# Queries and keys loaded apart, FFN units woven in halves, and TensorE in the program's order

## The chip, the cores and the metric

The kernel runs on one core of a Trainium2 chip. A core has five engines that work side by side and meet at semaphores: TensorE (PE, matmuls; PEld is its loading of weights), VectorE (DVE), ScalarE (ACT), GpSimd (POOL) and SyncE (SP), which here only issues DMAs. Each engine takes its own instructions strictly in the order in which they were put into its queue: a waiting instruction holds up all that stand behind it. Matmul results land in PSUM, of which the program uses eight banks of 128 x 512 float32; everything else is in SBUF or, beyond the core, in HBM. The metric is the device time of one execution in microseconds (us).

## The reference

One layer over 2048 time steps of 1024 channels, all in float32:

```python
h = _rmsnorm(x, g_attn)
p = h @ w_in                      # parts a_b, a_c, a_h, b_glu, q, k, v
y_a = a_b * _causal_dwconv(a_c * a_h, w_conv_a)
g = b_glu[..., :256] * jax.nn.sigmoid(b_glu[..., 256:])
y_b = jax.nn.silu(_layernorm(_causal_dwconv(g, w_conv_b) + b_conv_b, ...))
y_c = _stick_breaking(q, k, v)    # 8 heads of 64
x = x + jnp.concatenate([y_a, y_b, y_c], axis=-1) @ w_out
h2 = _rmsnorm(x, g_ffn)
x = x + jnp.square(jax.nn.relu(h2 @ w_ff1)) @ w_ff2
return _rmsnorm(x, g_final)
```

Stick-breaking attention has no softmax. With the scores z = q k / 8, a key s < t gets the weight sigmoid(z[t, s]) times the product of sigmoid(-z[t, r]) over the keys r between s and t. The kernel needs running products over keys, from the latest backwards.

## The kernel before, in words

Every float32 product is made of three faster ones: a factor is split into a rounded high part and the rest (lo), and TensorE adds high x high, lo x high and high x lo. `mm3` (lines 99 to 107) emits these, so lines 103, 105 and 107 stand for all large products; PSUM tiles tell them apart (ps_p input projection, ps_x output projection, ps_u first FFN product, ps_y second, ps_z scores, ps_o attention's output).

Time runs along the free axis in four blocks of 512 steps (TB). The first part, up to about 600 us, makes the input projection, the two convolution mixers and the attention of block 0, and writes keys and queries to HBM (KQ) and values (VS). The second part is four calls of `block(tb, ...)`: output projection (eight tiles ps_x, 24 matmuls each), the norm, then 32 units `ffn1` (24 matmuls each) and, after every four of them, `ffn2` (eight tiles ps_y of 12 matmuls). Weights come in pieces through buffers w1 (four pieces, two units) and w2 (three); block 0 splits w1 and stores the parts, block 1 does so for w2, and later blocks load them.

Attention for block i + 1 runs beside block i. `attention` (line 702) is a generator over groups (head h, block i). It mixes two passes, one step at a time: `a_pass1` of a group and `a_pass2` of the group before. A step of pass 1 makes one PSUM tile of scores (ps_z), two sigmoids on ACT, and products on POOL and DVE. The first three steps are the diagonal block, made from `Kd`, the block's own keys, with masks on POOL (`a_diag`); then come 4 i steps with the earlier keys `Kl`, which have one buffer and whose load is issued at the head's first step. `a_cross_a` (line 603) then makes the running products across partitions: a transposition of 32 x 32 squares into T, a scan into O, small products C, and a product back into T. A step of pass 2 multiplies a tile A0 with transposed products (ps_q), splits it into Ahi (ACT) and Alo (POOL), and two steps later issues the matmuls with values into ps_o (`a_av`, lines 691 to 700).

`weave` (line 57) sets how the two mix. Main generators yield their cost (5.2 per unit of 24 matmuls, 2.6 per ps_y tile), and after each yield the side generator is driven on to a share of its own cost (0.5 per step) that grows from 0 at `t0` = 45 to its whole at `t1` = 365 or 320. So in the program's text attention's instructions stand in clumps between units. That text is only a priority: a scheduler, which runs a model of the timeline, then fixes each engine's queue, taking ready instructions first by priority (`high_priority` moves some forward). The order on the chip is fixed before it runs.

`a_load` (line 489) brings KQd: a tile of three parts (keys, high queries, low queries), issued on POOL's queue, with one buffer (`KQd=1`); in `attention` it is called after a group's loop has ended. In `block`, lines 955 to 966 take the column sum of squares (ps_ss) by TensorE, form mt on DVE, spread it by TensorE over partitions (ps_R), copy it to ms, and scale the eight tiles acc by it before the first `ffn2` adds to them.

## Time and profile before

| what | value |
|---|---|
| median of 3 runs | 2451.35 us (2446.44 to 2455.63) |
| the profiled execution | 2458.28 us, its span 2456.6 us |
| mean granted TensorE clock | 0.990 of full speed |
| instructions in the span | 32414 |
| data moved | 549.05 MB, 224 GB/s on the mean |
| HBM read and written | 390.38 MB and 148.11 MB |

A row of a group reads: line, engine, operation, what it writes and reads, shapes and count; then busy time and mean time of one in ns; then the idle time of the engine before it and what ended that. A windows row gives, for a stretch of the span, its length, the busy time of PE, PEld, DVE, ACT and POOL with the number of instructions, the granted TensorE clock (1.00 is full speed), the share of the 16 DMA engines that was busy, and GB/s. A timeline row gives start and duration in us. A busy TensorE need not be at its peak, since matmuls overlap in their records.

### The profile page before, as it was taken

The numbers are of one execution on the slowest core, as the hardware profiler recorded it, in microseconds if no ns is written. First come the engines' busy times: TensorE is split into PE (matmuls) and PEld (weight loads), VectorE is DVE, ScalarE is ACT, GpSimd is POOL, SyncE is SP. The second block draws the span as 40 slices with busy tenths as digits, with TensorE's granted clock in tenths as the row PEclk, the third lists the DMA queues.
The fourth block names the chain that finished last, engine by engine and source line by source line (L and its number), as shares of the span: only waits on it lengthen the run. The fifth ranks groups of instructions, "written<-read, shape, count | busy, mean of one in ns | idle before, by whom it ended". The sixth has DMA issues, their size and how long they took to land.

```text
span 2456.6 us, 32414 instructions
## 1 busy us (share of the span) xinstructions
PE 2395.6 (98%) x11316; PEld 2017.3 (82%) x11316; DVE 1627.6 (66%) x2348; ACT 1033.6 (42%) x1910; POOL 1163.9 (47%) x1221
## 2 busy tenths in 40 slices
PE   8999998999999999999999999999999999999998
PEld 7889876898778878787878888888888888888887
DVE  7957799943988878767977768677666735212114
ACT  5232522333566556534545555345555532121121
POOL 1342576641667666515666677158888830000000
PEclk9999999999999999999999999999999999999999
DMA  7579977888688878687778777776666656655555
GB/s 262 189 257 333 298 247 208 239 280 265 161 244 226 230 196 211 175 287 234 218 211 250 241 231 212 243 240 190 183 204 194 199 178 204 242 195 186 200 187 189
DMA packets 236036, 549.05 MB, mean 224 GB/s; under 512 B 25696, under 2 KB 99424, under 8 KB 217440
## 3 DMA queue, kind: packets, MB, share of 16 engines
q1 hardware_dynamic: 162896, 464.11, 54.8%
q0 software_dynamic: 53888, 73.42, 15.8%
q10 hardware_dynamic: 19088, 9.44, 1.3%
q8 instruction: 90, 1.47, 0.2%
q14 instruction: 74, 0.61, 0.1%
HBM read 390.38 MB, written 148.11 MB: 219 GB/s over the span
## 4 chain that ended last, share of the span: by engine, by line
PE 81%; DVE 9%; DMA 6%; issue 2%; ACT 1%; POOL 1%; POOLq 0%; SPq 0%; DVEq 0%; ACTq 0%
PE ps_y L103 8%; PE ps_y L107 8%; PE ps_y L105 8%; PE ps_u L103 8%; PE ps_u L105 8%; PE ps_u L107 8%; PE ps_p L107 4%; PE ps_p L105 4%; PE ps_p L103 4%; DMA KQd<-KQ 2%; PE ps_z L515 2%; PE ps_x L103 2%; PE ps_x L105 2%; PE ps_x L107 2%; PE ps_z L516 2%; DMA w<-s_w 2%
## 5 line engine op out<-in xcount | busy, mean ns | idle before, releaser
L90 POOL TENSOR_TENSOR Alo<-A,Ahi 128x512 fp32r<-128x512 f32 x288 | 394.3, 1380 | 105.7 <-PE ps_o L700 45.9
L944 DVE TENSOR_TENSOR acc<-acc,ps_y 128x512 f32<-128x512 f32 (+1 forms) x264 | 174.8, 666 | 178.0 <-PE ps_y L107 176.6
L103 PE MATMUL ps_y<-fh,w 128*128 128x512 f32 (+1 forms) x1056 | 282.9, 386 | 6.9 <-DVE acc L944 4.5
L103 PE MATMUL ps_u<-hh,w 128*128 128x512 f32 x1024 | 280.2, 394 | 7.7 <-DMA w<-s_w 4.8
L107 PE MATMUL ps_y<-fl,w 128*128 128x512 f32 (+1 forms) x1056 | 279.6, 385 | 1.0 <-DVE fl L919 1.0
L105 PE MATMUL ps_y<-fh,w 128*128 128x512 f32 (+1 forms) x1056 | 279.6, 385 | 0.0
L105 PE MATMUL ps_u<-hh,w 128*128 128x512 f32 x1024 | 278.0, 393 | 0.0
L595 POOL TENSOR_TENSOR A<-A,R 128x512 f32<-128x512 f32 x168 | 232.5, 1385 | 93.7 <-ACT A L593 69.6
L107 PE MATMUL ps_u<-hl,w 128*128 128x512 f32 x1024 | 276.6, 391 | 0.0
L909 ACT ACTIVATE ps_u<-ps_u 128x512 f32<-128x512 f32 x128 | 74.7, 584 | 460.0 <-PE ps_u L107 460.0
L118 POOL TENSOR_TENSOR rs_y<-rs_v,mhalf 128x4 f32<-128x4 f32 (+1 forms) x13 | 14.9, 1149 | 522.0 <-DVE rs_v L117 485.1
L103 PEld LDWEIGHTS ps_y<-fh,w 128*128 128x128 f32 x1056 | 193.2, 188 | 46.7 <-DVE acc L944 4.9
L103 PEld LDWEIGHTS ps_u<-hh,w 128*128 128x128 f32 x1024 | 191.5, 190 | 47.2 <-DMA w<-s_w 6.1
L107 PEld LDWEIGHTS ps_y<-fl,w 128*128 128x128 f32 x1056 | 195.6, 189 | 40.6 <-DVE fl L919 1.6
L105 PEld LDWEIGHTS ps_u<-hh,w 128*128 128x128 f32 x1024 | 194.3, 190 | 41.4 <-DVE w L90 0.2
L105 PEld LDWEIGHTS ps_y<-fh,w 128*128 128x128 f32 x1056 | 195.4, 188 | 39.7
L107 PEld LDWEIGHTS ps_u<-hl,w 128*128 128x128 f32 x1024 | 193.1, 189 | 40.2
L88 ACT ACTIVATE Ahi<-A 128x512 fp32r<-128x512 f32 x288 | 177.5, 628 | 92.9 <-PE ps_o L699 37.0
L919 DVE TENSOR_TENSOR fl<-ps_u,fh 128x512 fp32r<-128x512 f32 x128 | 87.5, 685 | 194.6 <-ACT fh L918 194.2
L597 DVE TENSOR_TENSOR R<-ps_z,R 128x512 f32<-128x512 f32 x168 | 115.4, 687 | 147.8 <-ACT ps_z L594 108.9
L452 DVE SCALAR_TENSOR_TENSOR ps_c<-g,wb,ps_c 128x512 f32<-128x512 f32 x240 | 179.8, 749 | 4.8
L88 ACT ACTIVATE w<-wraw 128x512 fp32r<-128x512 f32 x152 | 92.1, 628 | 182.4 <-PE ps_y L107 115.8
(173 smaller groups left out, 4952.2 us busy)
## 6 DMA issues: line engine op xcount, KB each, us to landing
w<-s_w SPq DMA_DIRECT2D x200, 512.0 KB, 3.5
w<-s_w SPq DMA_DIRECT2D x68, 1024.0 KB, 4.8
wraw<-in_w SPq DMA_DIRECT2D x192, 256.0 KB, 4.9
w<-s_w_out SPq DMA_DIRECT2D x64, 512.0 KB, 4.8
s_w<-w SPq DMA_DIRECT2D x32, 1024.0 KB, 5.5
s_w<-w SPq DMA_DIRECT2D x56, 512.0 KB, 5.2
KQd<-KQ POOLq DMA_DIRECT2D x64, 384.0 KB, 7.1
xraw<-in_xT SPq DMA_DIRECT2D x48, 256.0 KB, 4.8
```

Source lines behind the costliest of these rows:

```text
L88: nc.scalar.activation(hi, x, AF.Copy)
L90: e.tensor_tensor(lo, x, f(hi), op=ALU.subtract)
L103: self.nc.tensor.matmul(ps, wh, xh, start=start and k == 0, stop=False)
L105: self.nc.tensor.matmul(ps, wl, xh, start=False, stop=False)
L107: self.nc.tensor.matmul(ps, wh, xl, start=False, stop=stop and k == n - 1)
L452: nc.vector.scalar_tensor_tensor(t, g[:, k : k + TB], self.wb[:, c, k : k + 1], t, op0=ALU.mult, op1=ALU.add)
L515: nc.tensor.matmul(z[:, oc], keys, g["qh"][:, qc], start=k == 0, stop=False)
L595: nc.gpsimd.tensor_tensor(t, t, R, op=ALU.mult)
L597: nc.vector.tensor_tensor(Rn, z, R, op=ALU.mult)
L909: nc.scalar.activation(ps, ps, AF.Relu)
L919: nc.vector.tensor_tensor(lo, ps, f(hi), op=ALU.subtract)
L944: nc.vector.tensor_tensor(acc[d][:, cols], acc[d][:, cols], ps, op=ALU.add)
```

## The change

It has five edits.

1. `a_load` becomes `a_queries` (tile Qd, two buffers, loads issued on SP's queue) and `a_keys` (tile Kd, one buffer, still on POOL's queue). In `attention` the next group's queries are loaded once the present group has made one step of pass 1, its keys once it has made three.
2. The diagonal products of keys stay in the tile om instead of going to a tile Rd, and are transposed in two halves of 256 columns into T, as soon as each exists. The scan runs in place in T, and the tile O is gone. T1, the diagonal's T, has two buffers in the first part and one in the blocks.
3. `ffn1` yields after each half of a unit (12 matmuls, cost 2.6).
4. In `block` the third unit, `ffn1(2)`, is emitted between the column sum and the spread.
5. The four blocks are built in a region in which TensorE issues its instructions in the order in which the program emits them. The other engines' order, and TensorE's order outside the region, stay the scheduler's.

```diff
-    def a_load(self, h, i):
-        q0 = TB * i
-        pool = self.at
-        g = {"h": h, "i": i}
-        t = pool.tile([P, 3, TB], F32R, name="KQd", tag="KQd", bufs=self.ab["KQd"])
+    def a_queries(self, h, i):
+        q0 = slice(TB * i // 2, TB * i // 2 + TB // 2)
+        q = self.at.tile([P, 2, TB], F32R, name="Qd", tag="Qd", bufs=2)
         for rows, kq in self.kq_halves(h):
-            to = t[rows].rearrange("c a (j q) -> c (a j) q", j=2)
-            self.load_r(to, kq.rearrange("c a j q -> c (a j) q")[:, :, q0 // 2 : (q0 + TB) // 2])
-        g["Kd"], g["qh"], g["ql"] = t[:, 0], t[:, 1], t[:, 2]
-        return g
+            self.dma(q[rows].rearrange("c a (j q) -> c (a j) q", j=2), kq[:, 1:3].rearrange("c a j q -> c (a j) q")[:, :, q0])
+        return {"h": h, "i": i, "qh": q[:, 0], "ql": q[:, 1]}
+
+    def a_keys(self, g):
+        q0 = slice(TB * g["i"] // 2, TB * g["i"] // 2 + TB // 2)
+        g["Kd"] = self.at.tile([P, TB], F32R, name="Kd", tag="Kd", bufs=1)
+        for rows, kq in self.kq_halves(g["h"]):
+            self.load_r(g["Kd"][rows].rearrange("c (j q) -> c j q", j=2), kq[:, 0, :, q0])
...
-        nc.vector.tensor_tensor(Rd[:, lo], om[:, lo], om[:, hi2], op=ALU.mult)
+        nc.vector.tensor_tensor(om[:, hi2], om[:, lo], om[:, hi2], op=ALU.mult)
+        T = pool.tile([P, 16, 33], F32, name="T", tag="T1", bufs=ab["T1"])
+        nc.gpsimd.memset(T[:, :, 32:33], 0.0)
+        nc.vector.transpose(T[:, 0:8, 0:32], om[:, hi2])
...
-        nc.vector.tensor_tensor(Rd[:, hi2], om[:, hi2], R[:, hi2], op=ALU.mult)
+        nc.vector.tensor_tensor(om[:, hi2], om[:, hi2], R[:, hi2], op=ALU.mult)
+        nc.vector.transpose(T[:, 8:16, 0:32], om[:, hi2])
...
-        O = pool.tile([P, 16, 33], F32, name="O", tag="O", bufs=1)
-        nc.vector.tensor_tensor_scan(fl(O), fl(T), fl(self.d1), 1.0, op0=ALU.mult, op1=ALU.add)
+        nc.vector.tensor_tensor_scan(fl(T), fl(T), fl(self.d1), 1.0, op0=ALU.mult, op1=ALU.add)
...
-                if not loaded and self.ab["KQd"] > 1 and d1 >= n1 / 2 and n + 1 < len(groups):
-                    nxt = self.a_load(*groups[n + 1])
-                    loaded = True
-            if not loaded and n + 1 < len(groups):
-                nxt = self.a_load(*groups[n + 1])
+                if nxt is None and d1 >= 1 and n + 1 < len(groups):
+                    nxt = self.a_queries(*groups[n + 1])
+                if nxt and "Kd" not in nxt and d1 >= 3:
+                    self.a_keys(nxt)
...
                     self.mm3(ps, [(*w(d), hh[d], hl[d]) for d in range(4 * q, 4 * q + 4)], start=q == 0, stop=q == 1)
+                    if q == 0:
+                        yield 2.6
...
-            yield 5.2 * len(cs)
+            yield 2.6 * len(cs)
...
+        yield from ffn1(2)
+        need2(2)
         ms = hp.tile([P, TB], F32, name="ms", tag="ss", bufs=2)
...
-        for c in range(2, FC):
+        for c in range(3, FC):
             yield from ffn1(c)
...
-                self.ab = dict(KQd=1, Kl=1, A0=6, om=2, R=1, Alo=2, Ahi=2, Vl=1, late=1, yc=2)
+                self.ab = dict(Kl=1, A0=6, om=2, R=1, T1=2, Alo=2, Ahi=2, Vl=1, late=1, yc=2)
...
-                self.ab = dict(KQd=1, Kl=1, A0=15, om=2, R=2, Alo=3, Ahi=3, Vl=2, late=2, yc=1)
+                self.ab = dict(Kl=1, A0=15, om=2, R=2, T1=1, Alo=3, Ahi=3, Vl=2, late=2, yc=1)
...
-                for tb in range(4):
-                    weave(self.block(tb, self.end), [(at, (74, 95, 107)[tb], 45, 365 if tb < 2 else 320, False)] if tb < 3 else [])
+                with tc.manual_schedule(engines={mybir.EngineType.PE}):
+                    for tb in range(4):
+                        weave(self.block(tb, self.end), [(at, (74, 95, 107)[tb], 45, 365 if tb < 2 else 320, False)] if tb < 3 else [])
```

More of the change, by code (lines that the diff above doesn't have):

```diff
@@ L552, in a_pass1 @@
         A0 = g["A0"] = []
-        Rd = new("Rd", 1)
         k2 = [g["Kd"][:, 0:P], g["Kd"][:, 256 : 256 + P]]
@@ L574, in a_pass1 @@
         nc.gpsimd.tensor_tensor(t, t, R, op=ALU.mult)
-        nc.vector.tensor_tensor(Rd[:, hi2], om[:, hi2], R[:, hi2], op=ALU.mult)
+        nc.vector.tensor_tensor(om[:, hi2], om[:, hi2], R[:, hi2], op=ALU.mult)
+        nc.vector.transpose(T[:, 8:16, 0:32], om[:, hi2])
         A0.append(t)
         yield 1
-        tot = self.a_cross_a(g, Rd, None)
+        tot = self.a_cross_a(g, T, None)
         if not i:
@@ L600, in a_pass1, with a_cross_a @@
             yield 1
-        self.a_cross_a(g, R, tot)
-    def a_cross_a(self, g, R, seed):
-        nc, pool = self.nc, self.at
-        T = pool.tile([P, 16, 33], F32, name="T", tag="T1" if seed is None else "T2", bufs=1)
+        T = pool.tile([P, 16, 33], F32, name="T", tag="T2", bufs=1)
         nc.gpsimd.memset(T[:, :, 32:33], 0.0)
         nc.vector.transpose(T[:, :, 0:32], R)
-        O = pool.tile([P, 16, 33], F32, name="O", tag="O", bufs=1)
+        self.a_cross_a(g, T, tot)
+    def a_cross_a(self, g, T, seed):
+        nc = self.nc
         fl = lambda x: x.rearrange("p a b -> p (a b)")[:, ::-1]
-        nc.vector.tensor_tensor_scan(fl(O), fl(T), fl(self.d1), 1.0, op0=ALU.mult, op1=ALU.add)
+        nc.vector.tensor_tensor_scan(fl(T), fl(T), fl(self.d1), 1.0, op0=ALU.mult, op1=ALU.add)
         C = self.tiny.tile([P, 16], F32, name="C", tag="C", bufs=3)
@@ L618, in a_cross_a @@
             s, d = slice(32 * a + 32, 32 * a + 64), slice(32 * a, 32 * a + 32)
-            nc.vector.tensor_tensor(C[d], C[s], O[s, :, 0], op=ALU.mult)
+            nc.vector.tensor_tensor(C[d], C[s], T[s, :, 0], op=ALU.mult)
         tot = None
@@ L622, in a_cross_a @@
             tot = self.tiny.tile([32, 16], F32, name="tot", tag="tot", bufs=2)
-            nc.vector.tensor_tensor(tot, C[0:32], O[0:32, :, 0], op=ALU.mult)
-        qt = T[:, :, 0:32]
-        nc.vector.tensor_tensor(qt, O[:, :, 1:33], C.unsqueeze(2).to_broadcast([P, 16, 32]), op=ALU.mult)
+            nc.vector.tensor_tensor(tot, C[0:32], T[0:32, :, 0], op=ALU.mult)
+        qt = T[:, :, 1:33]
+        nc.vector.tensor_tensor(qt, qt, C.unsqueeze(2).to_broadcast([P, 16, 32]), op=ALU.mult)
         g["qd" if seed is None else "ql"] = qt
@@ L703, in attention @@
         prev = None
-        nxt = self.a_load(*groups[0])
+        nxt = self.a_queries(*groups[0])
+        self.a_keys(nxt)
         for n in range(len(groups) + 1):
@@ L714, in attention @@
             lag = 0 if prev and prev["i"] else 2
-            loaded = False
             while live1 or live2:
@@ L730, in attention @@
                         live1 = False
-                if not loaded and self.ab["KQd"] > 1 and d1 >= n1 / 2 and n + 1 < len(groups):
-                    nxt = self.a_load(*groups[n + 1])
-                    loaded = True
-            if not loaded and n + 1 < len(groups):
-                nxt = self.a_load(*groups[n + 1])
+                if nxt is None and d1 >= 1 and n + 1 < len(groups):
+                    nxt = self.a_queries(*groups[n + 1])
+                if nxt and "Kd" not in nxt and d1 >= 3:
+                    self.a_keys(nxt)
             prev = g
```

## The prediction

> **What bounds the kernel now.** I read the page first: busy shares, then the chain that ended last.
>
> ```profile
> PE 2395.6 (98%) x11316; PEld 2017.3 (82%) x11316; DVE 1627.6 (66%) x2348; ACT 1033.6 (42%) x1910; POOL 1163.9 (47%) x1221
> PE 81%; DVE 9%; DMA 6%; issue 2%; ACT 1%; POOL 1%; POOLq 0%; SPq 0%; DVEq 0%; ACTq 0%
> PE ps_y L103 8%; PE ps_y L107 8%; PE ps_y L105 8%; PE ps_u L103 8%; PE ps_u L105 8%; PE ps_u L107 8%; PE ps_p L107 4%; PE ps_p L105 4%; PE ps_p L103 4%; DMA KQd<-KQ 2%; PE ps_z L515 2%; PE ps_x L103 2%; PE ps_x L105 2%; PE ps_x L107 2%; PE ps_z L516 2%; DMA w<-s_w 2%
> ```
>
> TensorE (PE) carries 81% of the chain. The number of its matmuls does not change, so the change can win only what TensorE loses: it stands idle for 2456.6 - 2395.6 = 61 us of the span, and it runs some stretches at a lower clock. One transfer has a place of its own in the chain: KQd, a head's block of queries and keys.
>
> Next I read the stages. The edits act mostly in the blocks, from 600 us on; attention ends near 2020. The first row is the windows view of that stage (length, then busy time per engine, granted clock, DMA share, GB/s), the others the waits of TensorE in it (total, times, longest).
>
> ```profile
> 600.00:2020.00 1420.00, 1389.70 (x6311) 1164.90 (x6310) 1056.31 (x1493) 742.71 (x1384) 893.91 (x936) 0.99 0.74 217
> PE ps_z L515 <- DMA KQd<-KQ: 15.2, 6, 5.5
> PE ps_y L103 <- DVE acc L944: 4.5, 4, 2.6
> PE ps_u L103 <- DMA w<-s_w: 3.6, 3, 2.1
> PE ps_u L103 <- DVE acc L944: 2.3, 1, 2.3
> PE ps_y L103 <- DVE fl L919: 2.2, 2, 1.6
> PE ps_y L107 <- DVE fl L919: 1.0, 2, 0.7
> ```
>
> So TensorE is idle for 30.3 us there, and half of it, 15.2 us, is one wait: the first scores of a head (ps_z) for KQd. Then the five windows around the longest of these waits:
>
> ```profile
> 710.00:730.00 20.00, 18.91 (x90) 15.56 (x89) 18.17 (x24) 9.32 (x17) 12.52 (x17) 1.00 1.00 229
> 800.00:820.00 20.00, 18.13 (x84) 15.31 (x83) 16.14 (x20) 10.68 (x20) 12.98 (x17) 0.91 0.68 187
> 880.00:900.00 20.00, 15.73 (x65) 12.72 (x64) 15.10 (x22) 10.65 (x21) 10.38 (x13) 0.91 1.18 252
> 1170.00:1190.00 20.00, 18.05 (x84) 15.37 (x83) 16.93 (x22) 7.96 (x16) 11.58 (x15) 0.91 1.03 238
> 1220.00:1240.00 20.00, 14.48 (x63) 12.07 (x62) 15.21 (x20) 7.09 (x14) 9.35 (x13) 0.88 1.04 296
> ```
>
> The idle times, 1.09 + 1.87 + 4.27 + 1.95 + 5.52 = 14.7 us, are nearly the whole wait. After four of the five the granted clock (0.91, 0.91, 0.91, 0.88) shows a second loss: (0.09 + 0.09 + 0.09 + 0.12) x 20 = 7.8 us of full-speed time, part of it while TensorE stood still anyway.
>
> **The change part by part.** *The loads.* Before, one buffer holds a head's keys and queries, so its load can be issued only when the previous head's last scores are done. The tile view of KQd (issue time, issue to landing) and one piece of the chain:
>
> ```profile
> L83 POOL DMA_DIRECT2D KQd<-KQ x64: 651/688/951, 188.9 to 1905.8; - x64
> DMA to landing us min/median/max: 4.4/7.1/16.8
> 1219.64 16.23 DMA KQd<-KQ
> ```
>
> After, the queries (two buffers) are asked for after the first step of the head before, and the diagonal keys (one buffer) after its third, when their last reader has been issued. A head with i = 1 has 7 first-pass steps, so at least four of them, over half a head, lie between the keys' load and their use, against a median landing of 7.1 us and a worst of 16.8. The waits in the windows at 800 and 880 belong to heads two apart, so a head spans some 40 us there, and half of one is 20. I therefore remove the wait whole: **15.2 us**, and **6 us** of the 7.8 of clock (bounds 0 and 7.8; nearer the upper, since the lowered clock follows the wait). The 64 query loads now go past SP's queue, among weight loads that wait for buffers; SP's own issue has 0% of the chain, and the queries have a whole head of lead. The 64 loads that stay on POOL's queue carry a third of the bytes; POOL's time for one is 0.69 us at most, as now.
>
> [...]
>
> *The tiles T, Rd and O.* The scan runs in place and the products stay in om. The count of DVE operations grows by one per head, since one transposition of 512 columns becomes two of 256:
>
> ```profile
> L608 DVE STREAM_TRANSPOSE T<-Rd 128x512 f32<-128x512 f32 x32 | 22.7, 708 | 0.8
> L944 DVE TENSOR_TENSOR acc<-acc,ps_y 128x512 f32<-128x512 f32 x248 | 168.2, 682 | 173.8 <-PE ps_y L107 172.9
> L944 DVE TENSOR_TENSOR acc<-acc,ps_y 128x256 f32<-128x256 f32 x16 | 6.7, 421 | 4.3 <-PE ps_y L107 3.7
> ```
>
> A half transposition is not in the trace. Bounds: nothing extra, or 0.71 us, a whole transposition. The nearest pair of sizes gives 2 x 421 - 682 = 160 ns, which I take. For the 24 heads of the blocks it lies beside a DVE that is idle for 26% of the stage (1056.31 of 1420). For the 8 heads of the first stage I let it count: 8 x 0.16 = **1.3 us**; at 0.71 it would be 5.7. If the cover in the blocks is gone, 24 x 0.16 = 3.8 more. The memset of T1's last column moves ahead of the head's second diagonal step. It and the keys' load can hold POOL:
>
> ```profile
> POOL T L607 <- DVE ps_q L643: 103.1, 45, 6.7
> POOL KQd L83 <- PE ps_z L516: 33.4, 6, 24.0
> ```
>
> Both waits exist already. Behind them on POOL stand the masks and the low halves (Alo), which the second matmul of attention (ps_o) needs two steps later. POOL is busy 893.91 of 1420 us, and no wait of TensorE for POOL is among the six largest, of which the smallest is 1.0 us, so I cost the move at nothing.
>
> *The third FFN unit before the spread.* In the program's order the spread of the norm would stand right behind the column sum that it needs; now 24 matmuls lie between. The scaling of acc then comes earlier than in the old trace, where fl came late behind it: of 2.2 + 1.0 us I take **2 us** (bounds 0 and 3.2).
>
> *TensorE in the program's order, and units in halves.* Inside a block the weave already hands out attention between units. Halves hand it out after 12 matmuls instead of 24, which evens the pieces; I give that nothing (bounds 0 and the 4.5 us that ps_y waits for acc). At the start of a block it matters: the weave gives no attention before 45 units of work, and the output projection is 8 x 5.2 = 41.6, yet the trace shows attention there, put by the scheduler. The full windows at the start of the FFN of blocks 1 and 3, then ps_o's and ps_z's share at blocks 1 and 2:
>
> ```profile
> 1091.00:1124.00 33.00, 28.75 (x129) 23.48 (x128) 29.01 (x38) 14.81 (x27) 19.91 (x22) 0.90 1.00 325
> 2092.00:2112.00 20.00, 18.55 (x89) 15.45 (x88) 8.66 (x15) 5.37 (x9) 0.00 (x0) 1.00 0.82 318
> 1091.00:1124.00 33.00, 4.71 (x20) 3.13 (x20) 0.00 (x0) 0.00 (x0) 0.90 1.00 325
> 1597.00:1619.00 22.00, 2.01 (x7) 1.32 (x7) 0.68 (x1) 0.59 (x1) 1.00 0.81 309
> 1091.00:1124.00 33.00, 3.32 (x18) 3.13 (x18) 0.69 (x1) 3.13 (x6) 0.90 1.00 325
> 1597.00:1619.00 22.00, 1.93 (x6) 1.53 (x6) 0.73 (x2) 3.18 (x6) 1.00 0.81 309
> ```
>
> This filling, at most 4.71 + 3.32 + 2.01 + 1.93 = 12 us, moves to later. Where TensorE would have waited for weights without it, the wait returns. Bounds: a loss of 12 us (all of it uncovered), or a gain of the 4.25 us that block 1 loses now, since its key and query loads leave a stage in which the DMA engines are at 1.00. Block 3 has no filling and loses 1.45 us at this place; I take that for block 2 and no change for block 1: a loss of **1.5 us**.
>
> *Sum.* 15.2 + 6 + 2 - 1.3 - 1.5 = 20.4 us. The profiled execution took 2458.28 us (span 2456.6 and 1.7 around it), 6.9 above the median of the runs shown; it would become 2437.9. Taken off the median: 2451.35 - 20.4 = **2431 us**.
>
> **The rivals.** *The weights become the wait.* In the five windows DMA runs at 0.68 to 1.18 of its engines; the weight loads landed later between 600 and 1300 us (first row) than over the whole run (second):
>
> ```profile
> w<-s_w SPq DMA_DIRECT2D x41, 512.0 KB, 6.6
> w<-s_w SPq DMA_DIRECT2D x200, 512.0 KB, 3.5
> ```
>
> If TensorE only runs on to the next late weight, two thirds of 15.2 + 6 come back as waits of ps_u and ps_y: the gain is 20.4 - 14.1 = 6 us, 2445. For it: four of five windows have DMA at 1.00 or more. Against it: the weights have two units of buffers, and the stage's mean is 0.74. [...]
>
> *The filling is missed.* All 12 us uncovered instead of 1.5: a gain of 9.9 us, 2441, within the measurement.
>
> *Slower: earlier keys (Kl) hold TensorE.* They keep one buffer, and in the program's order the first scores with them block everything behind. One head with i = 3: the last score of the head before, the first diagonal and the first Kl score (PE); the issues of KQd and Kl (POOL); Kl's landing:
>
> ```profile
> 1845.99 0.39 PE L516 MATMUL ps_z<-KQd,Kl 128*128 128x512 f32 x1
> 1855.54 0.28 PE L515 MATMUL ps_z<-KQd 128*128 128x256 f32 x1
> 1860.10 0.50 PE L515 MATMUL ps_z<-KQd,Kl 128*128 128x512 f32 x1
> 1847.00 1.35 POOL L83 DMA_DIRECT2D KQd<-KQ  x2
> 1848.34 1.21 POOL L83 DMA_DIRECT2D Kl<-KQ  x2
> DMA to landing us min/median/max: 8.5/9.7/11.0
> ```
>
> Kl's second half, issued at about 1848.9, lands 11.0 us later at the longest, 1859.9: 0.2 us before its use. Without KQd ahead it is issued 1.35 us sooner, which is why I cost it at nothing. If the first Kl score comes 2 us too early in the 16 heads with i = 2 and 3, TensorE loses 32 us: 2451.35 - 20.4 + 32 = 2463, and with the clock loss per wait seen above (1.8 us) 2492. It decides from a mean lateness of 20.4 / 16 = 1.3 us. I name 2470.
>
> *More is won.* If the even pieces also take away the other waits of the stage (30.3 - 15.2 = 15.1, less the 2 counted), the time is 2418.
>
> That the order changes nothing beyond the loads would give 15.2 + 6 - 1.3 = 19.9 us, 2431 too; the time alone can't tell it.
>
> **How the numbers follow.** Chances: forecast 0.50, more won 0.10, weights 0.16, filling 0.10, slower 0.14. A measurement here can tell 0.5%, 12.3 us, from no change: faster means below 2439.1, slower above 2463.6. Of the forecast's 0.50 I leave 0.04 to "same", since the first stage's order is made anew by the scheduler and DVE there may give or take some us; of the weights' and the filling's 0.26, 0.08 go to faster. Faster: 0.46 + 0.10 + 0.08 = 0.64; same: 0.04 + 0.18 = 0.22; slower 0.14. The range goes from 2408 (more won, with block 1's 4.25 and the rest of the clock and fl terms) to 2460, which leaves out most of the slower case. The forecast's own is 2420 to 2440.
>
> **What would show it.** Right: no TensorE wait of a diagonal ps_z for queries or keys; clock 1.00 where those windows lie; Qd and Kd landing tens of us before use; no attention matmul in the output projections. Wrong: ps_z waiting for Kl at heads with i = 2 and 3; waits of ps_u or ps_y for w in the blocks above 3.6 us by the amount won; idle time at 1091 growing by what filled it. I would be wrong outright if ps_o waited for Alo again and again, POOL being held by T1's memset or by the keys' load.

## The result and the profile after

| | before | after |
|---|---|---|
| median | 2451.35 us (2446.44 to 2455.63) | 2485.14 us (2480.08 to 2492.46, 5 runs) |
| profiled execution | 2458.28 us, span 2456.6 | 2485.14 us, span 2483.4 |
| mean granted clock | 0.990 | 0.985 |

The ratio is 1.0145, with a 95% interval of 1.0128 to 1.0162: the change makes the kernel 34 us slower. The forecast was 20 us faster, and the time lies outside the range.

From the page of the kernel after, the chain that ended last, by engine and by line:

```profile
PE 57%; DVE 9%; DMA 4%; issue 2%; POOL 1%; ACT 1%; SPq 0%; DVEq 0%; POOLq 0%; ACTq 0%
PE ps_y L103 8%; PE ps_y L107 8%; PE ps_y L105 8%; PE ps_u L103 7%; PE ps_u L105 7%; PE ps_u L107 7%; DMA w<-s_w 3%; DVE A L659 2%; PE ps_z L518 2%; PE ps_z L519 2%; PE ps_x L103 2%; PE ps_x L105 2%; PE ps_x L107 1%; PE ps_o L706 1%; PE ps_o L705 1%
```

The queries' load (KQd, 2% before) has left the chain, as forecast. In its place stand the weights (3%) and a VectorE line, `A L659`: the product of an attention tile with ps_q, which the second pass of a head makes. The longest waits of TensorE from 600 to 2020 us, after (total, times, longest):

```profile
PE ps_y L103 <- DVE fl L927: 16.1, 5, 5.5
PE ps_y L107 <- DVE fl L927: 6.4, 4, 3.6
PE ps_u L103 <- DMA w<-s_w: 6.4, 6, 2.5
PE ps_x L103 <- DVE acc L868: 4.2, 2, 2.1
PE ps_z L518 <- DVE R L603: 4.1, 2, 3.5
PE ps_o L697 <- DVE yc L680: 2.2, 3, 1.1
```

The 15.2 us for KQd are gone. But `fl`, the low half of an FFN unit, made by VectorE, went from 2.2 + 1.0 to 16.1 + 6.4 us. Five windows that the prediction or the waits name, after (length, busy time per engine, clock, DMA share, GB/s); the first is the stage:

```profile
600.00:2020.00 1420.00, 1376.60 (x6218) 1150.12 (x6217) 1048.12 (x1511) 745.39 (x1375) 895.59 (x935) 0.98 0.71 213
710.00:730.00 20.00, 20.00 (x93) 16.71 (x92) 18.09 (x26) 12.12 (x22) 14.64 (x17) 1.00 0.87 210
880.00:900.00 20.00, 20.00 (x95) 16.79 (x94) 13.59 (x19) 11.34 (x21) 11.69 (x13) 1.00 0.94 226
1045.00:1065.00 20.00, 17.90 (x80) 14.74 (x79) 8.14 (x13) 3.74 (x6) 1.04 (x1) 0.91 0.68 221
1091.00:1124.00 33.00, 31.48 (x150) 25.91 (x150) 23.84 (x34) 16.15 (x31) 19.02 (x21) 1.00 1.02 318
```

Where KQd was waited for, TensorE is now full and its clock 1.00; at 1091 it is fuller than before (31.48 against 28.75 us). Over the stage it still lost: idle time is 43.4 us, where it was 30.3. The place of the loss is the last third, 1600 to 2140 us, before and then after:

```profile
1600.00:2140.00 540.00, 537.46 (x2444) 451.96 (x2443) 328.62 (x482) 244.14 (x446) 309.49 (x304) 1.00 0.65 202
```

```profile
1600.00:2140.00 540.00, 517.71 (x2290) 431.88 (x2290) 324.81 (x473) 240.39 (x438) 307.71 (x305) 0.97 0.60 184
```

In the same 540 us TensorE gets 154 matmuls less done; at the 227 ns of an undisturbed one (before, twelve in 2.72 us from 569.72 us on) that is some 35 us, an estimate. It is more than the 26.9 us between the two profiled executions, since the kernel after was ahead when this stretch began (the table below has the stages). Idle time gives 537.46 - 517.71 = 19.8 us of it; the lowered clock (0.97) gives about 0.03 x 540 = 16 us.

One such loss step by step. VectorE's timeline after, from the start of block 2's FFN (start, duration, line, what it makes, count, idle time before it):

```profile
1600.35 4.05 DVE L969 SCALAR_TENSOR_TENSOR em<-mt 128x4 f32<-128x4 f32 x1
...
1609.87 10.59 DVE L975 TENSOR_TENSOR acc<-acc,ms 128x512 f32<-128x512 f32 x7 [0.77 <-ACT ms L973]
...
1628.96 7.25 DVE L659 TENSOR_TENSOR A<-A,ps_q 128x512 f32<-128x512 f32 x12
1636.13 0.68 DVE L927 TENSOR_TENSOR fl<-ps_u,fh 128x512 fp32r<-128x512 f32 x1
```

TensorE's timeline after at that moment:

```profile
1631.32 0.40 PE L519 MATMUL ps_z<-Qd,Kl 128*128 128x512 f32 x1
1636.86 2.07 PE L103 MATMUL ps_y<-fh,w 128*128 128x512 f32 x4 [5.14 <-DVE fl L927]
1638.73 1.91 PE L105 MATMUL ps_y<-fh,w 128*128 128x512 f32 x4
1640.44 1.61 PE L107 MATMUL ps_y<-fl,w 128*128 128x512 f32 x4
1641.88 0.40 PE L705 MATMUL ps_o<-Ahi,Vl 128*128 128x512 f32 x1
...
1642.36 0.40 PE L518 MATMUL ps_z<-Qd,Kl 128*128 128x512 f32 x1
```

`fl` stands behind twelve attention products. It is also the last reader of a PSUM tile of ps_u, and the new ps_y tile needs that bank: ps_u and ps_y take turns in the same three banks, and the wait stands at line 103, which takes only fh. So TensorE waits 5.14 us, with matmuls of attention (ps_o, ps_z) right behind the waiting one in its queue. The first of these, at 1641.88, is held by its place alone: its values (Vl, issued at 1614.55) had landed by about 1624, and ACT had written the Ahi that it reads by 1630.3:

```profile
1629.66 0.63 ACT L88 ACTIVATE Ahi<-A 128x512 fp32r<-128x512 f32 x1 [0.34 <-DVE A L659]
```

The next twelve matmuls start over 1641.88 - 1636.86 = 5.0 us instead of the 2.7 of full speed: one wait of 5.1 us costs over 7.

VectorE came there late. Its seven scalings of acc took 10.59 us and the small `em` before them 4.05. Not every scaling was slow: one of the seven took more than half of the time, where an undisturbed one takes 0.68 us.

```profile
1613.01 5.83 DVE L975 TENSOR_TENSOR acc<-acc,ms 128x512 f32<-128x512 f32 x1
```

In run 1 below, which keeps all edits but the order, VectorE's timeline has at the same place:

```profile
1606.71 4.97 DVE L975 TENSOR_TENSOR acc<-acc,ms 128x512 f32<-128x512 f32 x8 [0.93 <-ACT ms L973]
...
1623.02 7.24 DVE L659 TENSOR_TENSOR A<-A,ps_q 128x512 f32<-128x512 f32 x12
...
1630.52 0.67 DVE L927 TENSOR_TENSOR fl<-ps_u,fh 128x512 fp32r<-128x512 f32 x1
```

and TensorE's, for the same ps_y tile:

```profile
1632.25 0.40 PE L705 MATMUL ps_o<-Ahi,Vl 128*128 128x512 f32 x1
...
1633.89 1.08 PE L103 MATMUL ps_y<-fh,w 128*128 128x512 f32 x4
```

All eight scalings take 4.97 us together, fl ends 5.6 us earlier (1631.2 against 1636.8), and seven matmuls of attention, from 1632.25 on, stand ahead of the ps_y tile that stand behind it in the kernel after. TensorE waits for nothing. So two things meet in the kernel after: VectorE is late, and the order has no work at that point to cover it. At this tile the lateness is the larger part. In run 1 fl is done before the seven matmuls start, and they last only 1633.89 - 1632.25 = 1.6 us of the 5.14. In run 7 below, which keeps the order but has no scaling held up, the same tile waits 1.14 us:

```profile
1633.34 1.19 PE L103 MATMUL ps_y<-fh,w 128*128 128x512 f32 x4 [1.14 <-DVE fl L927]
```

Nor does the order as such make the scalings late. In run 1 the eight at the start of block 0 take 12.28 us (from 635.90 on), and the mean of its 32 scalings is 1106 ns, as in the kernel after. The last section has what the traces show beside the slow ones. So this tile shows how a wait arises, but not what the order costs in all; that is in runs 1 and 13.

### The profile page after: what moved, and what is told of

It is laid out like the page before. It is cut to its first block, busy times and chain, and to the rows that moved or that the text cites. A ratio compares the mean times of both kernels' runs of the same rounds, so it can differ in the third digit from the quotient of the medians.

```text
span 2483.4 us, 32560 instructions
## 1 busy us (share of the span) xinstructions
PE 2408.5 (97%) x11316; PEld 2023.8 (81%) x11316; DVE 1617.8 (65%) x2380; ACT 1040.8 (42%) x1910; POOL 1163.8 (47%) x1221
## 4 chain that ended last, share of the span: by engine, by line
PE 57%; DVE 9%; DMA 4%; issue 2%; POOL 1%; ACT 1%; SPq 0%; DVEq 0%; POOLq 0%; ACTq 0%
PE ps_y L103 8%; PE ps_y L107 8%; PE ps_y L105 8%; PE ps_u L103 7%; PE ps_u L105 7%; PE ps_u L107 7%; DMA w<-s_w 3%; DVE A L659 2%; PE ps_z L518 2%; PE ps_z L519 2%; PE ps_x L103 2%; PE ps_x L105 2%; PE ps_x L107 1%; PE ps_o L706 1%; PE ps_o L705 1%
## 5 line engine op out<-in xcount | busy, mean ns | idle before, releaser
L103 PE MATMUL ps_y<-fh,w 128*128 128x512 f32 (+1 forms) x1056 | 282.9, 389 | 16.6 <-DVE fl L927 16.1
L118 POOL TENSOR_TENSOR rs_y<-rs_v,mhalf 128x4 f32<-128x4 f32 (+1 forms) x13 | 14.7, 1132 | 540.6 <-DVE rs_v L117 503.9
L103 PEld LDWEIGHTS ps_y<-fh,w 128*128 128x128 f32 x1056 | 194.9, 190 | 55.8 <-DVE fl L927 18.5
L105 PEld LDWEIGHTS ps_u<-hh,w 128*128 128x128 f32 x1024 | 193.2, 189 | 42.9 <-DVE w L90 1.5
L103 PEld LDWEIGHTS ps_u<-hh,w 128*128 128x128 f32 x1024 | 187.2, 189 | 48.1 <-issue 6.2
L90 DVE TENSOR_TENSOR w<-wraw,w 128x512 fp32r<-128x512 f32 x152 | 146.0, 979 | 29.9 <-ACT w L88 29.6
```

Source lines behind the costliest of these rows:

```text
L90: e.tensor_tensor(lo, x, f(hi), op=ALU.subtract)
L103: self.nc.tensor.matmul(ps, wh, xh, start=start and k == 0, stop=False)
L105: self.nc.tensor.matmul(ps, wl, xh, start=False, stop=False)
```

## The experiments

Every ratio is against runs of the kernel before that were taken beside it on the same chip (medians 2449.6 to 2451.6 us). Differences of medians below are not cleared of these 2 us between chips, so kernels that lie 5 us apart are told apart only where their intervals do not overlap (0.2% is 5 us).

| run | kernel | median, us | ratio, 95% interval |
|---|---|---|---|
| 1 | after, scheduler's order (edits 1 to 4) | 2451.29 | 1.0003 [0.9982, 1.0024] |
| 2 | before + order (edit 5) | 2565.07 | 1.0449 [1.0403, 1.0495] |
| 3 | before + edits 1 and 2 | 2461.71 | 1.0028 [1.0008, 1.0049] |
| 4 | after, `fl` given priority | 2485.04 | 1.0126 [1.0088, 1.0165] |
| 5 | before + edit 2 | 2461.92 | 1.0053 [1.0035, 1.0071] |
| 6 | after without edit 4 | 2479.95 | 1.0131 [1.0094, 1.0167] |
| 7 | after, acc scaled from PSUM | 2475.25 | 1.0112 [1.008, 1.0145] |
| 8 | run 1, acc scaled from PSUM | 2441.03 | 0.9954 [0.9934, 0.9973] |
| 9 | before, no DVE product | 2449.95 | 1.0004 [0.9987, 1.0021] |
| 10 | run 3, no DVE product | 2446.43 | 0.9977 [0.9957, 0.9996] |
| 11 | after, no DVE product | 2459.02 | 1.0029 [1.001, 1.0048] |
| 12 | run 1, no DVE product | 2435.72 | 0.9937 [0.9913, 0.9961] |
| 13 | order in blocks 0 and 1 only | 2446.13 | 0.9982 [0.9962, 1.0001] |
| 14 | run 5, two buffers of T1 | 2457.9 | 1.0043 [1.0027, 1.0059] |
| 15 | before + edit 1 | 2459.42 | 1.0044 [1.0028, 1.0061] |
| 16 | before, acc scaled from PSUM | 2448.46 | 1.0003 [0.9982, 1.0024] |
| 17 | run 13, acc scaled from PSUM | 2445.14 | 0.9976 [0.9959, 0.9994] |
| 18 | after, whole units | 2511.01 | 1.0245 [1.0204, 1.0287] |

To place the losses, I took from each trace the time from one matmul's start to the next, less its undisturbed pace (227 ns for 512 columns, as above; 120 ns for 256, as from 605.76 to 605.88 us in before, and taken for smaller ones too), and summed it by stage. "Start" of a block is its output projection and the first six FFN units. Waits and lowered clock are both in it.

```
us lost        first  block 0      block 1      block 2      block 3    tail   sum
               part   start rest   start rest   start rest   start rest
before         26.4    1.1  24.9    8.7  18.0    0.8   5.6    1.8  0.1   2.3   89.7
before+edit 1  28.4    3.4  17.2   11.8   6.8    6.5   7.3    0.9  0.0   2.3   84.6
before+edit 2  29.8    1.1  23.2    9.7   9.1    2.0  13.6    4.3  0.1   2.7   95.6
before+1+2     27.8    4.0  11.6   12.1   8.2    2.4  17.4    2.0  0.1   2.6   88.2
run 1          28.6    9.7  13.0   13.1   6.7    1.3  10.6    1.3  0.1   2.5   86.9
after          23.5    9.2  14.3    7.5   7.2   15.5  26.5    8.4  0.2   3.8  116.1
run 7          28.2    8.0  13.4    6.7   8.0    8.4  24.5   10.3  0.1   3.4  111.0
run 13         23.0    8.9  14.2    7.5   8.5    0.6  10.6    2.0  0.2   2.3   77.8
run 18         28.7    7.1  11.9    8.6  14.3   15.7  46.4    6.5  0.3   3.8  143.3
run 8          29.9    1.8  10.8    6.4   6.0    1.4  10.9    2.0  0.4   2.4   72.0
```

The sums differ as the profiled executions do (after less before: 26.4 in the table, 26.9 in time). But each is one execution. That of before lies 6.9 us above its median, those of edit 1 alone and of edits 1 and 2 lie 5.5 and 4.5 below theirs, so differences of some 10 us between medians need not show in the table.

**Run 1: the scheduler's order.** What does edit 5 cost?

```diff
-                with tc.manual_schedule(engines={mybir.EngineType.PE}):
-                    for tb in range(4):
+                for tb in range(4):
```

> The change without its fifth edit: the four blocks are built outside the region, so TensorE's order is the scheduler's. Theory O (the order costs): in the program's order a ps_y that waits for fl on a DVE busy with attention holds everything behind it, while the scheduler had other matmuls ready; then the waits of ps_y for fl (23 us in the changed kernel) go back to the 3 us of before, the wait for KQd stays gone, and the time is 2425 to 2440. Theory D (DVE): the early loads and the products in om make attention's work on DVE come in bursts whatever TensorE's order; then fl stays late by over 15 us and the time stays at 2475 to 2490.

Measured 2451.29: the order costs 2485.14 - 2451.29 = 33.9 us, the whole of the slowdown, and the other four edits together change nothing that can be measured (-4 to +6 us by the interval). Neither theory had this time. The cost of the order goes, as Theory O has it, but the waits for fl do not: from 600 to 2020 us ps_y still waits 14.7 us for it at line 107 (the row below) and 0.9 at line 103, against 22.5 in the kernel after.

```profile
PE ps_y L107 <- DVE fl L927: 14.7, 6, 7.5
```

So the sum over this stage does not tell the two orders apart; run 13 shows what does.

**Run 2: the order alone.** The same lines added to the kernel before.

> The kernel before with the fifth edit alone (TensorE in the program's order in the blocks; KQd, whole units and the old tiles stay). Theory O: the wait for KQd stays at 15 us or grows, since no other matmul can go ahead of a late ps_z, and waits for fl come on top: 2490 to 2530. Theory D: near the kernel before, 2445 to 2465.

Measured 2565.07, 114 us slower, beyond Theory O's range. The longest of TensorE's waits, 600 to 2020 us:

```profile
PE ps_z L515 <- DMA KQd<-KQ: 71.3, 18, 16.6
```

The same late transfer costs 15.2 us under the scheduler's order and 71.3 in the program's. So the order multiplies what a late input costs. Edit 1 takes this wait away, and run 18 shows that the halves make the order cheaper as well.

**Run 3: the loads and the tiles.** Run 1 without edits 3 and 4.

```diff
-                    if q == 0:
-                        yield 2.6
...
-        yield from ffn1(2)
-        need2(2)
```

> The kernel before with edits 1 and 2 alone (queries and keys loaded apart and early, products in om, scan in place); whole units, spread at its old place, scheduler's order. Theory O: the prediction's term for the loads, 15.2 + 6 - 1.3 us, comes true here: 2425 to 2438. Theory D: slower than before, 2465 to 2490.

Measured 2461.71: not 20 us faster but about 10 slower (2 to 12 by the interval), outside both ranges. The two longest waits in the stage:

```profile
PE ps_z L518 <- DVE R L603: 5.4, 5, 2.4
PE ps_y L103 <- DVE fl L925: 4.1, 2, 2.8
```

The wait for the load is gone and nothing large stands there. In the table the rest of blocks 0 and 1 lost 42.9 us before and 19.8 here: the load's 15.2 us and its clock loss did come true, 23 us. They went again in the first part (+1.4), at the starts of blocks 0 to 2 (+7.9) and above all in the rest of block 2 (+11.8), there mostly in waits for VectorE. Set against run 1, edits 3 and 4 together win 10.4 us under the scheduler by the medians; the intervals of the two ratios overlap.

**Run 4: `fl` first.** The copies of a finished unit given high priority in the changed kernel, so that VectorE would take fl ahead of the products.

```diff
+            with self.tc.high_priority(offset=HP):
                 for c, ps in zip(cs, pus):
                     nc.scalar.activation(ps, ps, AF.Relu)
```

> The change with the evacuation of ps_u (three ACT operations and fl on DVE) under the scheduler's high priority, so that DVE's queue has fl ahead of attention's products; TensorE still in the program's order. Theory O, with fl's place on DVE as the cause: the waits of ps_y for fl fall from 23 us to under 8, the clock rises from 0.985 to 0.99, and the time is 2445 to 2465. If it stays within 5 us of 2485, the place of fl on DVE is a symptom, and something else holds TensorE.

Measured 2485.04, no change. VectorE's order at 1629 came out the same: twelve products, then fl. The run does not test the theory, since the edit did not move what it was to move.

**Runs 5, 14 and 15: what edits 1 and 2 do one by one.** Run 5 has the tiles alone (edit 2 on the kernel before). Run 15 has the loads alone, with one buffer of queries in the first part and 13 tiles A0 in the blocks, for space. Run 14 is run 5 with

```diff
-A0=15, om=2, R=2, T1=1,
+A0=15, om=2, R=2, T1=2,
```

> The kernel before with edit 2 alone (products in om, transposed in halves, scan in place, T1 taken early); KQd, whole units, old spread, scheduler's order. Theory T (the tiles' edit costs what the loads win): 2465 to 2475, so that the loads alone would have given 2435 to 2440. Theory B (backlog: the wait for KQd only covered DVE's and POOL's lateness, which shows as soon as the wait is gone): no change from before, 2446 to 2457, with ps_z's wait for KQd still about 15 us.

> The kernel before with the loads of queries and keys apart, without the edit of the tiles. For the space it has one buffer of queries in the first part and 13 tiles A0 instead of 15 in the blocks. Theory A (the loads by themselves win the predicted 15 to 20 us and the tiles' edit eats them): 2430 to 2440 us. Theory B (the wait taken away is replaced by waits for VectorE whatever the tiles do): 2446 to 2456. No wait of the diagonal scores for queries or keys in either.

> The kernel before with the edit of the tiles T, Rd and O alone, and in the blocks two buffers of T1 instead of one. The tiles' edit alone gave 2461.9 us, 10 to 12 above before. Theory A (T is now written two steps earlier, so its memset on GpSimd waits for the last reader of the former head's T, 47 us in the blocks, with masks behind it): with a second buffer this wait goes, and 2449 to 2455 us come back. Theory B (the cost comes from the scheduler's changed order or the halved transpositions): stays at 2458 to 2464.

Run 5: 2461.92. The tiles' edit alone costs 12 us, though the two half transpositions take about what I had estimated. The groups of VectorE in the kernel after, beside the 708 ns of a whole one before:

```profile
L581 DVE STREAM_TRANSPOSE T<-om 128x256 f32<-128x256 f32 x32 | 14.2, 443 | 0.9
L564 DVE STREAM_TRANSPOSE T<-om 128x256 f32<-128x256 f32 x32 | 13.9, 435 | 0.2
```

443 + 435 - 708 = 170 ns a head, 160 foreseen. So the cost is not the instructions' own time. Run 14 (2457.9) was to take away one explanation, the earlier wait for the buffer T1, but it did not: GpSimd waits at that line as long as in run 5. Its waits for T there from 600 to 2020 us, in run 5 and in run 14:

```profile
POOL T L560 <- DVE ps_q L646: 47.4, 20, 4.9
```

```profile
POOL T L560 <- DVE ps_q L646: 48.0, 19, 5.3
```

So that explanation stays untested, and the 4 us between the two runs lie within their intervals. Run 15: 2459.42, 10 us slower also without the tiles' edit, with KQd's wait gone, and above both ranges. So the loads do not hold a 20 us gain that the tiles eat; each of the two edits, and both together, end 10 to 12 us above before by the medians (2 to 17 by the intervals). The scheduler orders every engine anew for each of these kernels. That this new order is the cost would fit, but no run shows it, and since the profiled executions do not reproduce the difference of medians, where these 10 us lie stays open.

**Run 6: the third unit back behind the spread** (edit 4 undone in the changed kernel).

```diff
-        yield from ffn1(2)
-        need2(2)
...
-        for c in range(3, FC):
+        for c in range(2, FC):
```

> The change without edit 4: the spread stands right behind the column sum again, and acc is scaled before the third FFN unit's results. If the scaling's new place is what makes ps_y wait in the first ffn2 of a block (waits of 5.5 and 5.1 us at 635 and 1636 in the changed kernel), these two go and the time falls by 10 us or more, against 1 to 2 us that TensorE waits for mt in each block: 2468 to 2478. If the place is innocent: 2485 to 2492.

Measured 2479.95, between the two ranges. The longest wait of ps_y for fl at line 103 fell from 5.5 to 2.5 us, but the time hardly. In the program's order edit 4 wins nothing; that it costs 5 us is not shown, since the interval of this run's ratio (1.0094 to 1.0167) holds that of the kernel after (1.0128 to 1.0162).

**Runs 7, 8, 16 and 17: the scaling of acc from PSUM.** The rows at 1609.87 and 1613.01 above show seven scalings in 10.59 us, one of them of 5.83. They read two SBUF tiles, acc and the copy ms. This edit takes the spread norm from PSUM instead:

```diff
-        ms = hp.tile([P, TB], F32, name="ms", tag="ss", bufs=2)
-        nc.scalar.activation(ms, self.spread(mt, "z"), AF.Copy)
+        ms = self.spread(mt, "z")
```

> The change with the eight scalings of acc reading the spread factor from PSUM, where TensorE left it, instead of from a copy in SBUF that ACT makes. In the changed kernel one such scaling takes about 1.5 us at 1610 while POOL works, where other DVE operations of this size take 0.68. If two SBUF operands are what makes DVE slow beside POOL, a scaling takes about 0.68 us, the eight end some 6 us sooner, the waits at 635 and 1636 shrink by most of their 10.6 us, and the time is 2470 to 2479. If the slowness has another cause, a scaling keeps 1.2 us or more and the time stays within 4 us of 2485.

> The same edit on the change without the program's order (TensorE's order is the scheduler's; that kernel took 2451 us). With the scaling at 0.68 us: 2438 to 2447, faster than before and after both. With a scaling that stays slow: 2449 to 2455.

> The kernel before, with the eight tiles acc scaled by the spread norm directly from PSUM and not from its copy in SBUF. With the scheduler's order and all edits but the order this was worth 10 us (2451.3 to 2441.0). [...] Theory B (it counts only where the other edits have made VectorE late): 2448 to 2454.

> The changed kernel with TensorE in the program's order in blocks 0 and 1 only, and with the eight tiles acc scaled directly from PSUM. Order in blocks 0 and 1 alone gave 2446.1 us; scaling from PSUM gave 10 us both with the order everywhere (2485.1 to 2475.3) and with the scheduler's (2451.3 to 2441.0). Theory A (the two do not meet): 2433 to 2439 us, the fastest of all. Theory B (in the scheduler's blocks 2 and 3 the scaling was worth little, and its gain lay in blocks 0 and 1, where the order now already fills the gap): 2440 to 2446.

The 32 scalings in the tile view (shortest, median and longest in ns, then the first and the last start), in the kernel after and in run 7:

```profile
L975 DVE TENSOR_TENSOR acc<-acc,ms x32: 674/685/5831, 628.6 to 2142.7; 128x512 f32<-128x512 f32 x32
```

```profile
L974 DVE TENSOR_TENSOR acc<-acc,ps_R x32: 666/677/689, 632.3 to 2137.6; 128x512 f32<-128x512 f32 x32
```

The median hardly moves; the long ones are gone, and with them the mean falls from 1106 to 676 ns. By the medians this wins 9.9 us in the changed kernel and 10.3 under the scheduler (2451.29 to 2441.03); the order's own price stays 34.2 us. In the kernel before it wins nothing (2448.46, as Theory B has it), though the mean falls from 950 to 679 ns there too, and with the order in blocks 0 and 1 only 1 us (2445.14, again Theory B). So it is no gain by itself: by the table run 8 has it at the starts of blocks 0 and 1 (9.7 to 1.8 and 13.1 to 6.4 us), where run 1 had lost more than the kernel before. Run 8 is the fastest kernel that does the whole computation, 0.46% below before (interval 0.27 to 0.66%).

**Runs 9 to 12: less work for VectorE.** In the kernels before, of run 3, after and of run 1, the products that VectorE makes for the tiles of earlier keys:

```diff
             else:
-                nc.vector.tensor_tensor(t, t, Q, op=ALU.mult)
```

> The kernel before without DVE's products of A with ps_q at the earlier keys (the second pass's steps k >= 3; 192 operations of 0.68 us, 117 us of DVE; the attention weights of earlier keys then lack that factor). DVE falls from 66% to about 61%, TensorE's matmuls stay. It is the base for the next kernel. Theory B (TensorE waits for attention's lateness on DVE as soon as KQd no longer holds it): the wait for KQd stays near 15 us, the waits for DVE nearly vanish: 2430 to 2450.

> Edits 1 and 2 (loads apart and early, tiles) on the kernel without those products. With the products, edits 1 and 2 brought nothing (2461.7 against 2451.6). Theory B: with DVE relieved they bring 10 us or more against the kernel without products that has the old loads. Theory T (these edits cost by themselves, through TensorE's or POOL's work): the difference stays at 0 to 10 us slower.

> The whole change without those products. The program's order costs 34 us with them (2485 against 2451 with the scheduler's order). Theory B: most of this is TensorE standing before ps_y and ps_z until DVE has done attention's products; without them the order costs under 15 us against the next kernel. If the order costs by its own places (block starts, weights): still 25 us or more.

> The change without its fifth edit (scheduler's order) and without those products: the base for the kernel above. Theory B: 2420 to 2435, 15 us or more below the 2451 us with the products.

The kernel before gains nothing (2449.95): these products do not bound it, and its wait for KQd stays at 14.1 us. With the loads and the tiles, the same cut wins 15.3 us (2461.71 to 2446.43); in the changed kernel 26.1 (2485.14 to 2459.02), under the scheduler 15.6 (2451.29 to 2435.72). So with edits 1 and 2 these products of VectorE cost time, which they did not before. They are not the whole of the missing gain: without them edits 1 and 2 win 3.5 us (2449.95 to 2446.43), not the 10 or more of Theory B, and where the rest of the 20 us went stays open. The price of the order falls from 33.9 to 2459.02 - 2435.72 = 23.3 us, between the two forecasts (under 15, and 25 or more): about a third of it hangs on these products.

**Run 13: where the order costs.** The changed kernel, with the order in blocks 0 and 1 only:

```diff
-                with tc.manual_schedule(engines={mybir.EngineType.PE}):
-                    for tb in range(4):
+                for tb in range(4):
+                    with (tc.manual_schedule(engines={mybir.EngineType.PE}) if tb < 2 else ExitStack()):
```

> The changed kernel with TensorE in the program's order in blocks 0 and 1 only; in blocks 2 and 3 the scheduler's order. Theory A (the order costs its 34 us where heads with i = 3 are woven in and behind it, in blocks 2 and 3): 2447 to 2456 us, level with the scheduler's order everywhere (2451). Theory B (the order costs the same everywhere, and the later blocks only show what piled up): half of the 34 us stays, 2464 to 2472. If blocks 0 and 1 carry it: near 2485.

Measured 2446.13: 39.0 us faster than the changed kernel. It is also 5 us faster than the scheduler's order everywhere, but there the intervals overlap: in blocks 0 and 1 the program's order is level or a little better. All of its price arises from block 2 on. Heads with i = 3 (twelve steps with earlier keys, twelve products at a stretch on VectorE) are woven in there; that their length is the reason is not shown. In the table the start and rest of block 2 lose 42.0 us in the changed kernel and 11.2 here. The last third of this run:

```profile
1600.00:2140.00 540.00, 533.87 (x2414) 447.04 (x2413) 323.69 (x478) 237.99 (x431) 294.44 (x294) 1.00 0.62 196
```

TensorE's longest waits in these 540 us, in the kernel after and then in this run:

```profile
PE ps_y L103 <- DVE fl L927: 7.1, 2, 5.1
PE ps_y L107 <- DVE fl L927: 3.6, 1, 3.6
PE ps_z L518 <- DVE R L603: 3.5, 1, 3.5
PE ps_u L103 <- DMA w<-s_w: 2.9, 1, 2.9
PE ps_o L697 <- DVE yc L680: 2.2, 3, 1.1
```

```profile
PE ps_y L107 <- DVE fl L927: 1.7, 2, 1.4
PE ps_z L518 <- DVE R L603: 1.1, 1, 1.1
PE ps_u L103 <- DMA w<-s_w: 1.1, 1, 1.1
```

TensorE is idle for 540 - 517.71 = 22.3 us there in the kernel after and for 6.1 here, and the clock is 0.97 against 1.00, about 16 us. So the price consists in about equal parts of added waits (16.2 us) and of the lowered clock, together some 32 of the 39.0 us, an estimate since a low clock and a wait can fall together. With the rows that are not shown, 18.5 of the 22.3 us are waits for a result of VectorE, and 5.0 of the 6.1 here. No single wait carries it. How much of this is a result that comes later and how much a lack of other work beside it, these rows do not separate.

**Run 18: whole units** (edit 3 undone in the changed kernel).

```diff
-                    if q == 0:
-                        yield 2.6
...
-            yield 2.6 * len(cs)
+            yield 5.2 * len(cs)
```

> The changed kernel with whole FFN units (24 matmuls between two hand-outs of attention), everything else as changed. Theory A (the halves even the pieces and so help TensorE in the program's order): 2495 us or more. Theory B (what counts is VectorE's lateness, which the halves don't touch): 2480 to 2490. If the halves put attention's scores too close behind each other: below 2478.

Measured 2511.01, 25.9 us slower than with halves; the rest of block 2 loses 46.4 us instead of 26.5. In the program's order the size of the pieces matters; that TensorE then has nothing but the program's own mixture to bridge a late result is my reading of it.

## Why the prediction was wrong

- **The loads' wait** (15.2 us removed whole): right in the trace. No score waits for Qd or Kd. One reading beside it was wrong without harm: 0.69 us was the median of POOL's time for an issue, the longest 0.95; after, these are 0.62 and 0.79. The tile views of Qd and then Kd, after:

```profile
L79 SPq DMA_DIRECT2D Qd<-KQ x64: 573/608/1463, 188.6 to 1856.5; - x64
DMA to landing us min/median/max: 3.5/6.6/15.2
```

```profile
L83 POOL DMA_DIRECT2D Kd<-KQ x64: 590/618/792, 135.2 to 1868.8; - x64
DMA to landing us min/median/max: 2.6/5.0/8.0
```

- **The clock** (6 us): right at its places (1.00 at 710 and 880), lost again elsewhere (0.97 from 1600 to 2140). In the window at 1045 TensorE is idle for 2.1 us in all, in one wait of ps_x for acc, and the clock is 0.91.
- **The gain as a whole**: the first step that failed. Without the order the terms add up to 15.2 + 6 + 2 - 1.3 = 21.9 us; run 1 has just these edits and gains nothing that can be measured. 15.2 + 6 is what TensorE lost for the load, not what the kernel gains without it: runs 3 and 15 removed the wait and were 10 us slower. The table has 19 to 23 us won in blocks 0 and 1 and most of it given back, in waits for VectorE among others. To the question what is late next I had answered with the weights alone (their rival, 2445). VectorE, idle for 26% of the stage, I held for cover; the share of the stage hid that it is late in stretches, and runs 9 to 12 show that its products cost time once the loads are early and the tiles changed: leaving them out is worth nothing in the kernel before and 15 us with edits 1 and 2. They do not account for the whole gain that is missing; the rest is open.
- **The tiles** (1.3 us): the operation was sized right, 170 ns for 160. The edit by itself cost 12 us; the cause is open.
- **The third unit** (2 us): no gain in the program's order (run 6); fl's waits, which it should end, grew instead. It cannot be told apart from the halves under the scheduler, where both together win 10.4 us by the medians.
- **The program's order** (1.5 us lost, bounds -12 to +4.25): the step that decided the sign. I costed only what I could see move, attention's filling at the block starts, and took the order inside a block as equal because the weave hands out attention there anyway. Not costed was what a late input costs when its reader no longer stands where the scheduler expected the input: for one and the same load 15.2 us became 71.3 (run 2). The price is 33.9 us (run 1), where 1.5 had been forecast, and all of it arises from block 2 on (39.0 us, run 13), in about equal parts as waits, mostly for VectorE, and as the lowered clock. The two failed steps make up the whole distance from 2431 to 2485 us: 21.9 not won and 33.9 - 1.5 = 32.4 more lost. The window at 1091, where I saw the largest filling, got better.
- **The halves** (nothing, bounds 0 and 4.5): 25.9 us in the program's order (run 18), far outside the bounds.
- **The rivals.** Kl late under the program's order was the slower one: its way (one late input holds all that stand behind it) was right (71.3 us for KQd in run 2), its place was not. No wait for Kl is among the six longest of the stage; VectorE's fl, acc and R are. The weights did grow, from 3.6 to 6.4 us in the stage, which is too little to decide. The sign that I called wrong outright, ps_o held by Alo, did not come (once, 0.7 us in the stage). "That the order changes nothing beyond the loads" was put at 2431 too, and run 1's 33.9 us show how far that was off.

## What to carry to other kernels

TensorE's program order changed what a late input costs (15.2 us became 71.3 for one load), not only the places where the old trace shows work moved; I would now price it by listing, per stage, each producer that a TensorE instruction depends on and how late it runs at its worst, and try the order one stage at a time (here two blocks came out level and the other two lost 39 us). A stall that is removed need not be a gain (runs 3 and 15: 15.2 us of waits gone, 10 us slower), and a busy share of 74% over a stage says nothing about stretches of 20 us (VectorE in the kernel after: 18.09 of the 20 us from 710 on), so look at the other engines' timelines right behind the stall. The mean of a group says as little: 1106 ns stood for 18 scalings of under 0.7 us and 14 of 1.07 to 5.83. And where the profiled execution is 7 us off the median, terms of 5 to 20 us read from it need a second execution before they are added up.

## What the runs showed of the hardware that I had not expected

In these traces a VectorE operation with two SBUF operands is at times held while GpSimd works through several of its own. Above, a 128 x 4 operation took 4.05 us at 1600 us (0.16 in run 1), and one 128 x 512 scaling 5.83 at 1613 (0.68 undisturbed); GpSimd was busy for 4.00 and 5.79 us of these stretches. GpSimd's timeline after shows beside the first:

```profile
1600.57 1.30 POOL L90 TENSOR_TENSOR Alo<-A,Ahi 128x512 fp32r<-128x512 f32 x1
1601.83 1.30 POOL L601 TENSOR_TENSOR A<-A,R 128x512 f32<-128x512 f32 x1
1603.09 1.28 POOL L90 TENSOR_TENSOR Alo<-A,Ahi 128x512 fp32r<-128x512 f32 x1
```

The small operation ends, at 1604.40, as the third of these does (1604.37). Under the scheduler's order (run 1) VectorE and then GpSimd at the same place:

```profile
1601.22 0.16 DVE L969 SCALAR_TENSOR_TENSOR em<-mt 128x4 f32<-128x4 f32 x1
```

```profile
1614.98 1.24 POOL L83 DMA_DIRECT2D Kl<-KQ  x2 [8.08 <-PE ps_z L519]
```

There GpSimd happens to be idle for 8.08 us, and the eight scalings (1606.71 to 1611.68) fall into that gap; none takes over 0.76 us. The small operation at 1601.22 falls into another, of 3.06 us before 1602.52. In the kernel after GpSimd does nothing from 2137 to 2143 us, and the eight scalings of block 3, which lie there, take 0.68 to 0.69 each. So the traces show such an operation held, 5.83 against 0.68 us, and no scaling held with one operand from PSUM (0.69 us at the longest of 32 in run 7, where GpSimd is busy for 894.25 of the 1420 us of the stage, in which the first 24 lie). By the records the 128 x 4 operation starts at 1600.35, ahead of the first of the three GpSimd operations (1600.57), and ends behind the third. Why it is held, no run shows.

The other surprise is the clock: after a single wait of 5.14 us the next four matmuls took 0.47 us each from start to start ((1638.73 - 1636.86) / 4), half of full speed (the granted clock is 0.54 from 1636 to 1642), and full speed was back some 5 us later (four in 0.94 us from 1641.88 on).
